# A gated two-branch decoder block on one core: another order for the gate products, the y pieces and the last output rows

## The chip, the cores and the metric

The kernel runs on one core of a Trainium2 chip. The metric is the device time of one execution in microseconds (us); the number given for a kernel is the median of several runs. The engines are PE (matrix products, with PEld for its weight loads), DVE (vector), ACT (scalar, activation functions), POOL (GpSimd) and SP, which in this kernel only issues DMAs. Each engine works through its own queue in order.

## The reference

The input x has 1024 rows of 1024 values. It is normalised and projected, two attention branches are computed, and they are merged by gates, cut here to what matters:

```python
h = rms_norm(x, g_pre)
qa, ka, va, fa, za, qb, kb, vb, zb, gates = split(h @ w_in)
ya = fox_attention(qa, ka, va, log_sigmoid(fa + b_forget))      # 8 heads, "forgetting"
ya = ya * silu(za)
yb = diff_attention(rope(qb), rope(kb), vb, lam)                # 4 heads, "differential"
yb = rms_norm(yb, g_subln) * (1 - lam_init) * silu(zb)
gate_a, gate_b = split(sigmoid(gates))                          # 1024 each
merged = gate_a * (ya @ w_branch[0]) + gate_b * (yb @ w_branch[1])
y = merged @ w_out
out = x + rms_norm(y, g_post)
```

All is float32. The kernel gets the accuracy by splitting each operand into a high and a low part and taking three products (high-high, high-low, low-high), so a product of 128x128 by 128x512 costs three matmuls per 128 of depth.

## The kernel before

The work has five stages. First x is normalised and transposed into hT (high and low parts, four quarters `hT[part][kh][sh]`: two halves of the model width by two halves of the rows), and the two value projections are taken. Then the attention stage runs eight units (four differential, four forgetting), with the projections for the next unit, the z projections and the row sums of squares as filling; what it makes for later goes to DRAM: y_d (the attention outputs, eight tiles of 128 channels: 0 to 3 differential, 4 to 7 forgetting), z_d, rs_d (the scale of the inner norm) and t_d (four combinations of quarters of h). The diff touches the three stages after that.

**Gates.** The 16 column blocks of the gate projection are made in eight steps d. Step 0 is plain (`gates_plain`): 96 matmuls. Steps 1 to 7 (`gates_pair`) take one block of each gate together by Winograd's form of Strassen's product: seven products of half size (`wino`, 84 matmuls) in place of eight. The left operands are the quarters a11, a12, a21, a22 of the two weight blocks, loaded as `raw` (a pool of two buffers, so the next pair's loads wait until this pair's are read), or combinations S1 to S4 of them (`left_operands`, on POOL). Product 1 takes a11, 2 takes a12, 4 takes a22; 5 takes S1, 6 takes S2, 3 takes S4 and 7 takes S3. Each left operand is split into its parts by ACT (high) and DVE or, for products 2 and 4, POOL (low), into one of six operand slots in turn (`whi`, `wlo`, `wop`, two each). The right operands of products 1, 2, 3 are quarters of hT, and those of 4 to 7 are the T tiles, which `h_load` brings back from t_d (1 MB each, eight of them). `ORD` is the order in which the products are taken; pair 7 has an order of its own. As products finish, DVE adds them up in tiles of the tag "t" (eight buffers, `tmp`), ACT takes the sigmoid, and SP stores the result in g_d.

Between the pairs stand pieces of y * silu(z) (`y_work(t, c)`: tile t, half c of the rows; silu(z) is z times sigmoid(z)): a load of z and, for the differential tiles, of the inner norm's scale, into "t" tiles; one more DVE pass for the differential tiles; a product on POOL, a sigmoid on ACT and a product on DVE. `YORD[d]` lists the pieces that follow pair d. `y_load` brings y back from y_d.

**Branch.** `yT` holds y in two parts (ACT and DVE). For the forgetting branch first (groups 2 and 3, tiles 4 to 7), then for the differential one, 8 blocks of w_branch are taken against it: 384 matmuls. DVE and POOL multiply by the gates and add into `mg`, 128 x 8 x 1024. The slots of yT's first two groups and mg lie where the T tiles were.

**Output.** `out_pair(i)` makes the output rows of blocks i and i + 4 by seven products, for i = 0 to 3; pairs 0 and 1 are interleaved. The left operands are column blocks of mg, `mg[:, 4*kh:4*kh+4, (i+4*n)*P : (i+4*n+1)*P]`. A result of 512 columns goes to `out_half`: ACT sums its squares, POOL (DVE for rows 3 and 7) multiplies by g_post, and when a row block's second half is there, POOL makes the reciprocal root (`rstd_of`: scale and offset, then a power) and DVE makes result times root plus the residual x. The residual comes by a DMA of its own into one of two "ox" buffers, or for rows 3 and 7 into `lx`.

**What sets the order.** The text is a list, and a planner (`schedule_with_timeline_sim=True`) puts each engine's instructions in order ahead of time: by its own model of durations, an engine takes the ready instruction that stands first in the text. So instructions run out of the text's order where the planner found one ready earlier; on the chip the planned order of each queue is fixed, and an instruction that waits holds everything behind it in its queue. An example from the trace: the weights of pair 7 (L802) are issued at 737 and 740 us, ahead of the last z loads of pair 6 (L765).

The lines that the prediction names: L664 and L665 split a left operand (high, low), L677 combines, L706 adds, L713 multiplies, L760 loads y, L765 loads z, L769 to L772 are the y pieces, L776 stores a gate, L795 loads T, L802 loads raw, L837 casts yT, L848 is the branch product, L931 loads a residual, L939 and L936 multiply by g_post, L943, L112 and L113 make the root, L948, L949 and L951 finish a row.

Of the kernel before, what the change touches and what calls it, by code (L numbers as in the profile page):

```python
# [16 lines left out]
P = 128  # L17
S = 1024
D = 1024
# [11 lines left out]
YORD = ((), ((0, 0),), ((0, 1), (1, 0)), ((1, 1), (2, 0)), ((2, 1), (4, 0), (4, 1)),  # L31
        ((3, 0), (5, 0), (5, 1)), ((3, 1), (6, 0), (6, 1), (7, 0), (7, 1)), ())
# [14 lines left out]
def tile_hybrid_block(  # L47
# [742 lines left out]
    def h_load():  # L790
        for m in (6, 5, 7, 4):
            ts = [tpool.tile([P, 4, CH], F32R, tag=f"T{m}{part}", name=f"T{m}{part}")
                  for part in range(2)]
            for part in range(2):
                nc.sync.dma_start(f32(ts[part]), t_d[m][part])  # L795
            h_ops[m] = [[t[:, k, :] for k in range(4)] for t in ts]
# [122 lines left out]
    last = NB - 1  # L919
    lx = []  # L920

    def out_half(i, e, o, st):

        es = slice(e * CH, (e + 1) * CH)
        if i in (3, last):
            if not lx:
                lx.append(slot(hslot[1, 1][0], [P, 4, CH], F32, "lx"))
            xs = lx[0][:, (0 if i == 3 else 2) + e]
        else:
            xs = tmp.tile([P, CH], F32, tag="ox", name=f"ox{i}_{e}", bufs=2)  # L930
        nc.sync.dma_start(xs, x2[i * P:(i + 1) * P, es])  # L931
        ss = small.tile([P, 1], F32, tag="oss", name=f"oss{i}_{e}")
        nc.scalar.activation(gx[:, 1, 0:CH], o, AF.Square, accum_out=ss)
        if i in (3, last):
            g = tmp.tile([P, CH], F32, tag="t", name=f"go{i}_{e}")
            nc.vector.tensor_tensor(g, o, gp_bc[:, es], op=ALU.mult)  # L936
        else:
            g = o
            nc.gpsimd.tensor_tensor(g, o, gp_bc[:, es], op=ALU.mult)  # L939
        st.append((e, g, xs, ss))  # L940
        if len(st) == 2:
            rs = small.tile([P, 1], F32, tag="ors", name=f"ors{i}")
            nc.gpsimd.tensor_tensor(rs, ss, st[0][3], op=ALU.add)  # L943
            rstd_of(rs, rs, D, EPS)
            for e, o, xs, _ in st:
                es = slice(e * CH, (e + 1) * CH)
                if i == 3 and e == 0:
                    nc.scalar.activation(o, o, AF.Copy, scale=rs)  # L948
                    nc.gpsimd.tensor_tensor(o, o, xs, op=ALU.add)  # L949
                else:  # L950
                    nc.vector.scalar_tensor_tensor(o, o, rs, xs, op0=ALU.mult, op1=ALU.add)  # L951
# [63 lines left out]
```

## Time and profile before

| what | us |
|---|---|
| median of 3 runs | 958.73 (956.02 to 959.63) |
| profiled execution | 960.13 |
| its span, first to last instruction | 958.0 |
| PE busy | 900.7 (94%) |
| DVE busy | 627.2 (65%) |
| POOL busy | 489.6 (51%) |
| ACT busy | 437.0 (46%) |
| first matmul of the gates | 603.2 |
| first matmul of pair 1 | 625.1 |
| first matmul of the branch | 768.4 |
| first matmul of the output | 859.6 |
| end of the last matmul | 939.4 |

The mean granted clock of PE over the span is 0.982 of full speed.

How to read the lines. In a timeline a line is: start, length, engine, line of the kernel, operation, output <- inputs by the program's names, shape, count of instructions merged into the line, and in brackets how long the engine sat idle just before and what ended that. SPq is SP's queue: the time of a DMA's issue, with the landing later. In a table of stretches a line is: from:to, its length, busy time and count of PE, PEld, DVE, ACT and POOL, then PE's granted clock, the share of the 16 DMA engines that was busy, and GB/s. In a table of groups a line is: line, engine, operation, output <- inputs, count, busy us, mean ns of one, and idle time before with what ended it.

### The profile page before, as it was taken

To read this page: it belongs to the slowest core of one execution; us is meant where nothing else is said; L and a number is where in the kernel's file an instruction comes from. 1 tells how busy PE (TensorE), PEld (TensorE's weight loads), DVE (VectorE), ACT (ScalarE), POOL (GpSimd) and SP (SyncE) were. 2 spreads that over 40 slices of the span, in tenths; PEclk is the share of its full clock that TensorE was granted. 3 is DMA by queue.
4 is the path that set the end of the run, shared out by engine and by line. 5 is a ranking of instruction groups with operands and counts; after the bars stand their busy time and mean duration, and the time that the engine had idled before them with its cause. 6 is when DMAs were issued, how large, how long until landed. Compare 5 with 4: busy or idle time off the path is not lost.

```text
span 958.0 us, 13760 instructions
## 1 busy us (share of the span) xinstructions
PE 900.7 (94%) x4600; PEld 752.1 (79%) x4600; DVE 627.2 (65%) x1180; ACT 437.0 (46%) x862; POOL 489.6 (51%) x460
## 2 busy tenths in 40 slices
PE   7999989899999999999999988999999999999992
PEld 5999867787887888888878877777888768887871
DVE  7731258978768868578676478228665782559875
ACT  3521125665656574565745658323443550324331
POOL 7200035446545466464644575216655735878972
PEclk9999999999999999999999999998999989999997
DMA  9532454434334353534434350893445696210144
GB/s 314 193 110 91 142 134 114 105 80 123 97 94 138 95 155 116 154 122 130 143 123 136 103 186 28 325 377 122 139 138 172 186 370 203 73 38 1 48 150 154
DMA packets 115656, 136.95 MB, mean 143 GB/s; under 512 B 10609, under 2 KB 80241, under 8 KB 114562
## 3 DMA queue, kind: packets, MB, share of 16 engines
q1 hardware_dynamic: 115586, 136.08, 44.4%
q8 instruction: 36, 0.59, 0.3%
q14 instruction: 34, 0.28, 0.1%
HBM read 85.65 MB, written 37.81 MB: 129 GB/s over the span
## 4 chain that ended last, share of the span: by engine, by line
PE 58%; DVE 13%; POOL 8%; DMA 7%; issue 6%; ACT 5%; SPq 2%; DVEq 0%; POOLq 0%; ACTq 0%
PE x_g L713 11%; PE pv L195 9%; PE pb L848 9%; PE pz L246 7%; PE pk L246 4%; PE pq L246 3%; PE ypf L474 3%; PE pg L246 2%; PE ptf L450 2%; DMA swk<-rawk 2%; SPq L287 1%; DVE Pd L423 1%; PE ypd L474 1%; PE Sf L421 1%; DVE wo_op L890 1%
## 5 line engine op out<-in xcount | busy, mean ns | idle before, releaser
L195 PE MATMUL pv<-wvhi,hT 128*128 128x264 f32 (+2 forms) x384 | 89.3, 325 | 0.4 <-DVE hT L181 0.4
L246 PE MATMUL pk<-hT,hi_k 128*128 128x512 f32 x256 | 83.9, 401 | 4.2 <-DVE KB L298 2.4
L246 PE MATMUL pz<-hT,hi_z 128*128 128x512 f32 x256 | 85.1, 400 | 0.0
L848 PE MATMUL pb<-yT,hi_br 128*128 128x512 f32 x256 | 80.8, 398 | 1.9 <-ACT hi_br L232 1.6
L246 PE MATMUL pq<-hT,hi_q 128*128 128x512 f32 x256 | 82.3, 395 | 0.0
L713 PE MATMUL x_g<-T,a_g 128*128 128x512 f32 x336 | 79.5, 392 | 1.6 <-ACT a_g L664 1.2
L713 PE MATMUL x_o<-wo_op,a_o 128*128 128x512 f32 x336 | 77.4, 391 | 2.4 <-ACT a_o L664 1.2
L713 PEld LDWEIGHTS x_o<-wo_op,a_o 128*128 128x128 f32 x336 | 62.8, 188 | 16.9 <-ACT a_o L664 2.1
L713 PEld LDWEIGHTS x_g<-T,a_g 128*128 128x128 f32 x336 | 63.5, 190 | 15.7 <-ACT a_g L664 1.6
L195 PEld LDWEIGHTS pv<-wvhi,hT 128*128 128x128 f32 x384 | 64.6, 190 | 6.2 <-DVE hT L181 0.7
L542 POOL TENSOR_SCALAR Pf<-Pf,lf 128x1024 f32<-128x1024 f32 (+3 forms) x64 | 52.5, 824 | 30.2 <-DVE lf L430 27.4
L713 PE MATMUL x_g<-hT,a_g 128*128 128x512 f32 x252 | 62.0, 400 | 2.6 <-ACT a_g L664 2.0
L428 ACT ACTIVATE Pf<-Pf,mxf 128x1024 f32<-128x1024 f32 (+3 forms) x64 | 49.8, 778 | 32.1 <-DVE mxf L423 29.5
L428 ACT ACTIVATE Pd<-Pd,mxd 128x128 f32<-128x128 f32 (+7 forms) x64 | 49.5, 774 | 30.0 <-DVE mxd L423 28.2
L538 POOL TENSOR_TENSOR cb<-cb,trim 128x128 f32<-128x128 f32 x64 | 30.0, 470 | 62.9 <-DVE mxf L423 45.1
L195 PE MATMUL pv<-wvlo,hT 128*128 128x512 f32 (+2 forms) x192 | 61.9, 325 | 0.0
L512 POOL TENSOR_SCALAR Pd<-Pd,ld 128x128 f32<-128x128 f32 (+7 forms) x32 | 25.6, 799 | 68.8 <-DVE ld L511 38.2
L848 PEld LDWEIGHTS pb<-yT,hi_br 128*128 128x128 f32 x256 | 49.1, 193 | 13.1 <-ACT hi_br L232 2.0
L713 PEld LDWEIGHTS x_g<-hT,a_g 128*128 128x128 f32 x252 | 48.5, 193 | 13.7 <-ACT a_g L664 2.4
L246 PEld LDWEIGHTS pk<-hT,hi_k 128*128 128x128 f32 x256 | 47.6, 190 | 14.4 <-DVE KB L298 2.5
L454 DVE TENSOR_TENSOR plf<-ptf,phf 128x512 fp32r<-128x512 f32 (+1 forms) x80 | 49.6, 633 | 10.1 <-ACT phf L453 9.5
L246 PEld LDWEIGHTS pz<-hT,hi_z 128*128 128x128 f32 x256 | 47.9, 191 | 8.7
(243 smaller groups left out, 2426.6 us busy)
## 6 DMA issues: line engine op xcount, KB each, us to landing
t_d<-t SPq DMA_DIRECT2D x32, 256.0 KB, 2.2
T<-t_d SPq DMA_DIRECT2D x8, 1024.0 KB, 14.9
raw<-in_w_in_dram SPq DMA_DIRECT2D x14, 512.0 KB, 4.1
g_d<-c_g SPq DMA_DIRECT2D x21, 256.0 KB, 3.9
vb_d<-vbs SPq DMA_DIRECT2D x8, 512.0 KB
va_d<-vas SPq DMA_DIRECT2D x8, 512.0 KB, 3.8
raw_k<-in_w_in_dram SPq DMA_DIRECT2D x8, 512.0 KB, 5.3
raw_q<-in_w_in_dram SPq DMA_DIRECT2D x8, 512.0 KB
```

The costliest lines, as they stand in the source:

```text
L195: nc.tensor.matmul(ps[n], lhsT=hT[hp][k // 4][i // 4][:, k % 4, hs], rhs=wt[k][:, a:b], start=first, stop=(k == KT - 1 and hp == 1))
L246: nc.tensor.matmul(ps, lhsT=a[:, k, :], rhs=hT[h][k // 4][c][:, k % 4, :], start=(k == 0 and a is hi and h == 0), stop=(k == KT - 1 and a ...
L287: nc.sync.dma_start(sw[b * 32:(b + 1) * 32, :], raw[o * 32:(o + 1) * 32, :])
L428: nc.scalar.activation(pr[:, 0:n], pr[:, 0:n], AF.Exp, bias=mx[:, len(pcs) - 1:len(pcs)], scale=-1.0, accum_out=le)
L450: nc.tensor.transpose(pt[:, o * P:(o + 1) * P], rows[2 * g + r][:, j * P:(j + 1) * P], ident)
L454: nc.vector.tensor_tensor(pl[:, 0:n], pt[:, 0:n], ph[:, 0:n], op=ALU.subtract)
L474: nc.tensor.matmul(o, lhsT=a, rhs=b[:, src], start=(j == 0 and n == 0), stop=(odd == 1 and jj == g and n == len(prods) - 1))
L512: nc.gpsimd.tensor_scalar(p2[:, 0:n], p2[:, 0:n], l2, 1.0, op0=ALU.mult, op1=ALU.mult)
L538: nc.gpsimd.tensor_tensor(diag, diag, trim, op=ALU.add)
L542: nc.gpsimd.tensor_scalar(p1[:, 0:n], p1[:, 0:n], l1, 1.0, op0=ALU.mult, op1=ALU.mult)
L713: nc.tensor.matmul(x[m], lhsT=a[:, ai, k, :], rhs=right[m][bi][k], start=(k == 0 and n == 0), stop=(k == 3 and n == 2))
L848: nc.tensor.matmul(ps, lhsT=a[:, kk, :], rhs=yT[g][h][:, k % 2, sl], start=(k == 0 and a is hi and h == 0), stop=(k == 3 and a is lo))
```

## The change

Four things are changed.

- Pairs 1 to 6 take their products in the order 1, 2, 4, 6, 5, 7, 3 (`GATE`) in place of 1, 6, 5, 7, 2, 3, 4, and the T tiles are loaded in the order 4, 6, 5, 7. Pair 7 keeps its order. Because product 2 now comes before 6, the sum of products 1 and 2 gets a tile of its own instead of going over c11.
- The y pieces stand in another order and number: 2, 3 and 3 pieces of the forgetting tiles after pairs 1, 2 and 3, then 3, 3 and 2 of the differential tiles after pairs 4, 5 and 6. Before it was 1, 2, 2, 3, 3 and 5, differential first. All eight y loads stand before pair 1, the forgetting tiles first.
- The residual rows 2, 6, 3 and 7 are loaded, one DMA each, into columns of mg that output pairs 0 and 1 have read, and their loads stand in the text before pair 2. Rows 0, 4, 1 and 5 keep the two ox buffers.
- The last output pair takes 1, 6, 5, 7, 3, 4, 2 in place of 1, 6, 5, 2, 3, 7, 4. The norm's factor is moved: g_post is multiplied by the root of 1024 once, the first half's sum of squares gets the offset, and what is left behind the second half is one addition and one power. In row 3 it is the half that came first that ACT and POOL finish.

```diff
-YORD = ((), ((0, 0),), ((0, 1), (1, 0)), ((1, 1), (2, 0)), ((2, 1), (4, 0), (4, 1)),
-        ((3, 0), (5, 0), (5, 1)), ((3, 1), (6, 0), (6, 1), (7, 0), (7, 1)), ())
+YORD = ((), ((4, 0), (4, 1)), ((5, 0), (5, 1), (6, 0)), ((6, 1), (7, 0), (7, 1)),
+        ((0, 0), (0, 1), (1, 0)), ((1, 1), (2, 0), (2, 1)), ((3, 0), (3, 1)), ())
...
     def h_load():
-        for m in (6, 5, 7, 4):
+        for m in (4, 6, 5, 7):
...
+    GATE = (1, 2, 4, 6, 5, 7, 3)
     h_load()
     gates_plain(0)
-    for t in range(4):
+    for t in (4, 5, 6, 7, 0, 1, 2, 3):
         y_load(t)
     for d in range(1, KT):
-        if d == 4:
-            for t in range(4, 8):
-                y_load(t)
-        gates_pair(d, ORD if d < KT - 1 else (7, 5, 6, 4, 1, 2, 3))
+        gates_pair(d, GATE if d < KT - 1 else (7, 5, 6, 4, 1, 2, 3))
...
+    nc.gpsimd.tensor_scalar(gp_bc, gp_bc, math.sqrt(D), 1.0, op0=ALU.mult, op1=ALU.mult)
+    xres = {}
+
+    def residual(i, e):
+        if i % 4 < 2:
+            xs = tmp.tile([P, CH], F32, tag="ox", name=f"ox{i}_{e}", bufs=2)
+            nc.sync.dma_start(xs, x2[i * P:(i + 1) * P, e * CH:(e + 1) * CH])
+            return xs.rearrange("p (k n) -> p k n", k=4)
+        return xres[i][:, 4 * e:4 * e + 4]
+
+    def residual_early(i):
+        xs = mg[:, :, (i - 2) * P:(i - 1) * P]
+        nc.sync.dma_start(xs, x2[i * P:(i + 1) * P, :].rearrange("p (k n) -> p k n", k=KT))
+        xres[i] = xs
...
+        if not st:
+            nc.gpsimd.tensor_scalar(ss, ss, D * EPS, 0.0, op0=ALU.add, op1=ALU.add)
         st.append((e, g, xs, ss))
         if len(st) == 2:
             rs = small.tile([P, 1], F32, tag="ors", name=f"ors{i}")
             nc.gpsimd.tensor_tensor(rs, ss, st[0][3], op=ALU.add)
-            rstd_of(rs, rs, D, EPS)
-            for e, o, xs, _ in st:
+            nc.gpsimd.tensor_tensor(rs, rs, mhalf[:, 0:1], op=ALU.pow)
+            for n, (e, o, xs, _) in enumerate(st):
                 es = slice(e * CH, (e + 1) * CH)
-                if i == 3 and e == 0:
+                o4 = o.rearrange("p (k n) -> p k n", k=4)
+                if i == 3 and n == 0:
                     nc.scalar.activation(o, o, AF.Copy, scale=rs)
-                    nc.gpsimd.tensor_tensor(o, o, xs, op=ALU.add)
+                    nc.gpsimd.tensor_tensor(o4, o4, xs, op=ALU.add)
                 else:
-                    nc.vector.scalar_tensor_tensor(o, o, rs, xs, op0=ALU.mult, op1=ALU.add)
+                    nc.vector.scalar_tensor_tensor(o4, o4, rs, xs, op0=ALU.mult, op1=ALU.add)
                 nc.sync.dma_start(out2[i * P:(i + 1) * P, es], o)
...
     run_all(out_pair(0, OORD), out_pair(1, OORD))
+    for i in (2, 6, 3, 7):
+        residual_early(i)
     run_all(out_pair(2, ORD))
-    run_all(out_pair(3, (1, 6, 5, 2, 3, 7, 4)))
+    run_all(out_pair(3, (1, 6, 5, 7, 3, 4, 2)))
```

More of the change, by code (lines that the diff above doesn't have):

```diff
@@ L918, in tile_hybrid_block @@
     nc.sync.dma_start(gp_bc, g_post[0:1].to_broadcast([P, D]))
-    last = NB - 1
-    lx = []
+    nc.gpsimd.tensor_scalar(gp_bc, gp_bc, math.sqrt(D), 1.0, op0=ALU.mult, op1=ALU.mult)
[10 more added lines that the diff above has]
+        xres[i] = xs
     def out_half(i, e, o, st):
         es = slice(e * CH, (e + 1) * CH)
[L925 to L931, printed above, removed]
+        late = i % 4 == 3
+        xs = residual(i, e)
         ss = small.tile([P, 1], F32, tag="oss", name=f"oss{i}_{e}")
         nc.scalar.activation(gx[:, 1, 0:CH], o, AF.Square, accum_out=ss)
-        if i in (3, last):
+        if late:
             g = tmp.tile([P, CH], F32, tag="t", name=f"go{i}_{e}")
```

## Prediction

> **What bounds the kernel now.** I read the page first, for the engine that fills the span, then PE's own timeline from the gates on, since the diff touches nothing earlier, then the rows of the engines that end PE's waits.
>
> ```profile
> span 958.0 us, 13760 instructions
> PE 900.7 (94%) x4600; PEld 752.1 (79%) x4600; DVE 627.2 (65%) x1180; ACT 437.0 (46%) x862; POOL 489.6 (51%) x460
> ```
>
> PE has work for 94% of the span. So only the holes in PE's stream, and the end after its last matmul, are to be had.
>
> ```profile
> 625.14 2.88 PE L713 MATMUL x_g<-hT,a_g 128*128 128x512 f32 x12
> 646.30 0.83 PE L713 MATMUL x_g<-hT,a_g 128*128 128x512 f32 x2 [1.95 <-ACT a_g L664]
> 647.82 4.63 PE L713 MATMUL x_g<-hT,a_g 128*128 128x512 f32 x10 [0.69 <-DVE a_g L665]
> 669.24 2.88 PE L713 MATMUL x_g<-hT,a_g 128*128 128x512 f32 x12
> 688.27 2.88 PE L713 MATMUL x_g<-hT,a_g 128*128 128x512 f32 x12
> 746.76 0.73 PE L713 MATMUL x_g<-T,a_g 128*128 128x512 f32 x2 [1.20 <-ACT a_g L664]
> 768.39 1.21 PE L848 MATMUL pb<-yT,hi_br 128*128 128x512 f32 x4 [1.62 <-ACT hi_br L232]
> 859.63 11.04 PE L713 MATMUL x_o<-wo_op,a_o 128*128 128x512 f32 x48
> 917.62 21.81 PE L713 MATMUL x_o<-wo_op,a_o 128*128 128x512 f32 x94 [1.15 <-POOL a_o L665]
> ```
>
> These are PE's rows: start, length, and in brackets the wait before. Pair 1 starts at 625.14, pair 3 at 669.24, pair 4 at 688.27. An undisturbed pair is 688.27 - 669.24 = 19.03 us for 84 matmuls, 0.2266 us each. Pairs 1 and 2 took 44.10 us, not 38.06: **6.0 us lost** (A). Pairs 4 to 7 should end at 688.27 + 4 x 19.03 = 764.39, and the branch starts at 768.39: **4.0 us lost** (B), in pair 7 (746.76) and at the handover. The branch's 384 matmuls take 87.0 us at that pace and took 859.63 - 768.39 = 91.2: **4.2 us lost** (C). PE's last run ends at 917.62 + 21.81 = 939.4, and the span runs **18.6 us** on (D).
>
> ```profile
> 625.10:644.10 19.00, 19.00 (x85) 15.58 (x84) 4.84 (x7) 4.62 (x8) 2.58 (x2) 1.00 1.04 384
> ...
> 644.00:648.00 4.00, 1.35 (x5) 0.48 (x4) 2.42 (x3) 2.41 (x5) 3.34 (x3) 0.85 0.67 252
> 648.00:652.00 4.00, 4.00 (x10) 3.13 (x11) 4.00 (x4) 1.00 (x2) 3.37 (x3) 0.50 0.00 0
> 652.00:656.00 4.00, 4.00 (x16) 3.20 (x15) 3.27 (x3) 2.14 (x4) 4.00 (x3) 0.80 0.06 8
> 744.00:748.00 4.00, 2.41 (x10) 1.35 (x9) 1.26 (x2) 1.24 (x2) 3.15 (x3) 1.00 0.62 207
> 772.00:776.00 4.00, 4.00 (x11) 3.03 (x11) 4.00 (x4) 2.19 (x3) 2.37 (x1) 0.50 1.04 380
> ```
>
> In these stretches the last three figures are the granted clock, the DMA share and GB/s, and x after the second time counts PE's matmuls. After the waits at 644 and 768 the clock is half for some us: 26 matmuls in 648 to 656 where 35 fit (2.1 us lost), 11 in 772 to 776 where 18 fit (1.5 us). After the shorter wait at 745 it stays at 1.00. So A and C are part waiting, part slow clock.
>
> **Part 1: products 1, 2, 4 first.** What ends the wait of pair 2?
>
> ```profile
> 629.24 1.29 POOL L665 TENSOR_TENSOR a_g<-raw,a_g 128x512 fp32r<-128x512 f32 x1 [1.14 <-ACT a_g L664]
> 623.45 7.76 SPq L760 DMA_DIRECT2D yf<-y_d  x4
> 634.07 3.32 SPq L802 DMA_DIRECT2D raw<-in_w_in_dram  x2
> 644.58 1.27 POOL L677 TENSOR_TENSOR S_g<-raw 128x512 f32<-128x512 f32 x1 [14.05 <-DMA raw<-in_w_in_dram]
> 738.56 1.30 POOL L665 TENSOR_TENSOR a_g<-raw,a_g 128x512 fp32r<-128x512 f32 x1 [1.18 <-ACT a_g L664]
> 739.89 0.38 SPq L802 DMA_DIRECT2D raw<-in_w_in_dram  x1
> 744.77 1.28 POOL L677 TENSOR_TENSOR S_g<-raw,raw 128x512 f32<-128x512 f32 x1 [4.91 <-DMA raw<-in_w_in_dram]
> ```
>
> The next weights wait for the two raw buffers, and these come free with the splits of a12 and a22, products 2 and 4, which stand fifth and last. A split needs one of six operand slots, so product 4's waits for product 1 of its own pair: 629.24 in pair 1, 738.56 in pair 6. The load goes out behind it, 739.89, and lands 4.9 us later; pair 7 should have begun at 745.4. In front, the three splits that read raw directly need the slots of the second to fourth product of the pair before, done 10.9 us into that pair. So raw comes free some 8 us before its own pair starts instead of some 12 us after the start (738.56, where pair 6 began at 688.27 + 2 x 19.03 = 726.33): about 20 us more lead. In pair 1 the slots come free in the middle of the plain gates, about 614, so pair 2's weights go out behind the T loads and ahead of the yf loads, where they now go out after both. I estimate their landing at 632 to 636; they are needed at 644. The split counts, combinations and additions are the same in number. T4 is needed third instead of T6 second; the loads follow that order. One more "t" tile is held per pair (the sum p12 no longer overwrites c11), 5 of 8.
>
> **Part 2: the y pieces.** The forgetting tiles are the branch's first operands, and their pieces are now the last.
>
> ```profile
> 761.21 1.74 POOL L770 TENSOR_TENSOR yf<-yf,zs 128x512 f32<-128x512 f32 x1
> 763.51 3.88 ACT L837 CAST yT<-yf 128x1024 fp32r<-128x1024 f32 x4
> 767.30 1.04 ACT L232 CAST hi_br<-raw_br 128x1024 fp32r<-128x1024 f32 x1
> ```
>
> The last yf product at 761.21 holds ACT's four casts, these hold hi_br, and hi_br is PE's wait at 768.39. Done by pair 4 or 5, the casts are free from T's last use, four products into pair 7: 8.2 us before the end, against 3.88 + 1.04 us of ACT. What is loaded more: pairs 5 to 7 get three pieces of the differential kind.
>
> ```profile
> L665 DVE TENSOR_TENSOR a_g<-S_g,a_g 128x512 fp32r<-128x512 f32 x23 | 26.5, 1159 | 20.2 <-ACT a_g L664 20.2
> L706 DVE TENSOR_TENSOR c_g<-x_g,cu_g 128x512 f32<-128x512 f32 x10 | 6.8, 684 | 0.2
> L769 DVE SCALAR_TENSOR_TENSOR yd<-yd,gsub,rb 128x512 f32<-128x512 f32 x7 | 8.0, 1149 | 0.0
> L772 DVE TENSOR_TENSOR yd<-yd,zs 128x512 f32<-128x512 f32 x8 | 9.8, 1223 | 2.6 <-ACT zs L771 2.4
> ```
>
> DVE per such pair: 5 x 1.16 + 7 x 0.68 + 3 x (1.15 + 1.22) = 17.7 us under 19.03 us of PE. It is hidden, with 1.3 us to spare; without that cover each pair would cost what it runs over. Of A + B + C = 14.2 us I keep back 1.2 for a handover that is not seamless: **-13.0** (bounds: -14.2, and -2 if only pair 7's own 2 us go). Moving the y loads costs nothing: the planner put the yf loads at 623 already, far from their place in the text.
>
> **Part 3: residual rows and the last pair.**
>
> ```profile
> 937.38 0.33 SPq L931 DMA_DIRECT2D ox<-in_x_dram  x1
> 942.93 0.75 DVE L951 SCALAR_TENSOR_TENSOR cu_o<-cu_o,ors,ox 128x512 f32<-128x512 f32 x1 [3.95 <-DMA ox<-in_x_dram]
> 948.24 0.72 ACT L948 ACTIVATE go<-go,ors 128x512 f32<-128x512 f32 x1 [1.21 <-POOL ors L113]
> 949.04 1.27 POOL L949 TENSOR_TENSOR go<-go,lx 128x512 f32<-128x512 f32 x1 [0.83 <-ACT go L948]
> 950.96 0.68 DVE L706 TENSOR_TENSOR cu_o<-x_o,cu_o 128x512 f32<-128x512 f32 x1
> 952.82 0.19 POOL L112 TENSOR_SCALAR ors<-ors 128x1 f32<-128x1 f32 x1
> 953.68 1.42 DVE L951 SCALAR_TENSOR_TENSOR go<-go,ors,lx 128x512 f32<-128x512 f32 x2 [1.30 <-POOL ors L113]
> ```
>
> DVE stood 3.95 us for a residual row that could only be issued at 937.38, when one of two ox buffers came free; all additions of the last pair stand behind it in DVE's queue, and the very last one starts at 950.96, 11.5 us after PE is done. From it to the end are 7.0 us. With rows 2, 6, 3 and 7 in columns of mg that pairs 0 and 1 have done with, nothing of that waits: those columns are read before pairs 0 and 1 end, 859.63 + 168 x 0.2266 and 1.2 us of waits, so by 899, and the rows are needed after pair 2, which ends 19 us before 939.4. Their loads move 512 KB each in 512-byte chunks, as the raw loads do, which land 4.9 us after issue; the passes read mg in chunks of 128, as the combinations of pairs 0 to 3 do. In the new order product 2 is last and finishes only row 3. The end after the last addition: 7.0, less one small POOL step (0.28), plus the first half by ACT and POOL (0.80 + 1.27) in place of two DVE passes (1.42): 7.4. Row 7's two DVE passes may stand ahead of the last addition, 1.4 us more; with 0.2 of queueing I take 9.0 for the 18.6: **-9.6** (bounds: 7.4, -11.2; and 18.6, nothing). The scaling of g_post on POOL is one pass of 128x1024, by the row below 1.3 us; before the first output it lies in POOL's wait for ACT, and if not, costs that much once.
>
> ```profile
> L234 POOL TENSOR_SCALAR hi_k<-raw_k 128x1024 fp32r<-128x1024 f32 x8 | 10.1, 1267 | 48.3 <-DMA vb_d<-vbs 48.3
> ```
>
> Products 4 and 2, split by POOL, are now needed at about 934 and 937 while POOL sums rows 2 and 6: I set **+1** (0 to 3).
>
> Sum: 958.0 - 13.0 - 9.6 + 1.0 = 936.4 us of span; 2.1 us lie around the span (the profiled execution took 960.13): 938.5. The median shown, 958.73, is 1.4 below the profiled one: **937 us**.
>
> **A rule against a part of it.** The rows show half clock right behind 2.6 us of waiting with two matmuls between. The Trainium skill (TensorE: Matmul & The Clock Gate, "What's actually happening") has the clock fall only after an idle window of about 3.4 us. By the rule the slow stretches would not come from these waits and would stay, 941. The rows at 744 (1.00) and 648 (0.50) speak for the wait as cause, with a threshold below the one of the Trainium skill.
>
> **The rivals.** (1) Forecast: A to D mostly go, 937, own range 930 to 944: 0.58. (2) Pair 2's weights still land behind T and yf, since DMA moves 384 GB/s up to 644: A stays, 937 + 6 = 943: 0.10. For it: the queue is full throughout (DMA share 1.04). Against it: pair 2's issue would come ahead of 2 MB of yf. (3) The tail stays, because DVE's order, fixed ahead of time by the planner, puts the last additions behind row passes anyway: 937 + 9.6 = 947: 0.13. (4) The half clock has another cause and stays, 2.1 us at 648 and 1.5 at 772: 941: 0.03. (5) The written order is only a priority and the planner restores about the same execution: 954 to 959: 0.07. (6) Slower: head of line on SP. Three differential pieces ask for 6 tiles beside the 5 of a pair, 11 through 8 buffers; a z load that waits for one holds the next pair's weights behind it, and a pair stalls as pair 2 did, 6.0 us. With the old holes left and only the tail gained that is 950 + 6 per pair, over 963 from three pairs on; with four, 974: 0.09. Against it: raw is now ready about 20 us earlier, so it should stand ahead of those z loads.
>
> This kernel's measurement tells about 0.5%, 4.8 us, from no change. Faster: 0.58 + 0.10 + 0.13 + 0.03 = 0.84; same 0.07; slower 0.09. The range 930 to 950 holds cases 1 to 4.
>
> **What would show it.** Right: pair 2 follows pair 1 in 19.0 us with clock 1.00 from 644 on; raw issues before 623 for pair 2 and some 20 us ahead later; the branch's first wait under 1.2 us; no DVE wait on a residual; PE's end to the span's end 8 to 10 us. Wrong: waits on zs or t buffers in front of raw on SP, DVE without gaps in pairs 5 to 7, or the last additions still long after PE's end.

## The result and the profile after

The changed kernel takes **945.99 us** (median of 4 runs, 944.34 to 950.13); the kernel before took 958.97 beside it (956.02 to 959.63). The ratio is 0.988, with a 95% interval of 0.985 to 0.991: faster by 13.0 us, where the forecast was 937, 21.7 us faster, with a range of 930 to 950. The profiled execution took 945.37, 2.1 us more than its span, as before.

The head of the page after:

```profile
span 943.3 us, 13785 instructions
PE 895.5 (95%) x4600; PEld 750.5 (80%) x4600; DVE 625.4 (66%) x1180; ACT 435.8 (46%) x862; POOL 489.3 (52%) x461
```

PE's own timeline after: pair 1's start, pair 7 (second and third rows), the handover to the branch, the output.

```profile
625.85 5.60 PE L713 MATMUL x_g<-hT,a_g 128*128 128x512 f32 x24
...
740.09 11.04 PE L713 MATMUL x_g<-T,a_g 128*128 128x512 f32 x48
750.97 8.32 PE L713 MATMUL x_g<-hT,a_g 128*128 128x512 f32 x36
...
759.13 1.52 PE L846 MATMUL pb<-yT,hi_br 128*128 128x512 f32 x6
760.99 0.50 PE L846 MATMUL pb<-yT,lo_br 128*128 128x512 f32 x1 [0.34 <-POOL lo_br L236]
...
846.81 11.04 PE L713 MATMUL x_o<-wo_op,a_o 128*128 128x512 f32 x48
...
899.59 5.78 PE L713 MATMUL x_o<-wo_op,a_o 128*128 128x512 f32 x24 [1.36 <-POOL a_o L665]
906.28 22.03 PE L713 MATMUL x_o<-wo_op,a_o 128*128 128x512 f32 x94 [0.92 <-POOL a_o L665]
```

No row between 625.85 and 759.13 has a wait: seven pairs in 133.28 us are 19.04 each. The stages, cut at these rows (columns as in the prediction's table of stretches; the clock is the third figure from the end):

```profile
625.85:759.13 133.28, 133.28 (x590) 110.40 (x588) 94.65 (x104) 58.32 (x99) 78.10 (x53) 1.00 0.65 207
759.13:846.81 87.68, 87.34 (x386) 72.02 (x384) 47.00 (x53) 23.80 (x29) 57.78 (x31) 1.00 0.51 171
846.81:928.31 81.50, 77.85 (x337) 62.50 (x335) 66.39 (x64) 27.98 (x57) 64.20 (x52) 1.00 0.29 90
928.31:943.30 14.99, 0.01 (x1) 0.00 (x0) 8.12 (x12) 3.61 (x9) 3.20 (x7) 0.60 0.20 76
```

Beside the kernel before, whose cuts come from the prediction's rows in the same way:

| stage | before, us | after, us | measured | forecast |
|---|---|---|---|---|
| gates, pairs 1 to 7 (A, B) | 143.25 | 133.28 | -9.97 | -10.0 |
| branch (C) | 91.24 | 87.68 | -3.56 | -4.2 |
| output, to PE's last matmul (E) | 79.80 | 81.50 | +1.70 | +1 |
| end, from there on (D) | 18.57 | 14.99 | -3.58 | -9.6 |
| sum from pair 1 on | 332.86 | 317.45 | -15.41 | -22.8; -21.6 with the 1.2 kept back |

Pair 1 starts 0.7 us later; in the runs below it starts anywhere from 623.9 to 630.3. So stages are compared by their lengths.

The gates and the branch came out as forecast. Nearly two thirds of the gain at the end did not come. DVE's timeline at the end, after:

```profile
916.62 0.68 DVE L706 TENSOR_TENSOR cu_o<-x_o,cu_o 128x512 f32<-128x512 f32 x1
920.30 3.46 DVE L962 SCALAR_TENSOR_TENSOR c_o<-c_o,ors,mg 128x512 f32<-128x512 f32 x2 [3.00 <-POOL ors L954]
924.47 1.77 DVE L962 SCALAR_TENSOR_TENSOR c_o<-c_o,ors,mg 128x512 f32<-128x512 f32 x1 [0.71 <-POOL ors L954]
926.16 0.74 DVE L962 SCALAR_TENSOR_TENSOR cu_o<-cu_o,ors,mg 128x512 f32<-128x512 f32 x1
926.83 0.68 DVE L706 TENSOR_TENSOR cu_o<-x_o,c_o 128x512 f32<-128x512 f32 x1
...
934.31 1.42 DVE L962 SCALAR_TENSOR_TENSOR go<-go,ors,mg 128x512 f32<-128x512 f32 x2 [1.12 <-POOL ors L954]
935.64 0.69 DVE L706 TENSOR_TENSOR c_o<-x_o,c_o 128x512 f32<-128x512 f32 x1
```

The old wait for a residual (3.95 us) is gone; two shorter ones, of 1.25 us at 909.88 and 0.61 us at 912.44, stay in output pair 2, for rows that still come through an ox buffer. In place of the old one DVE stands 3.00 and 0.71 us for the roots of rows 2 and 6, which POOL makes, and the four finishing passes of these rows (L962) come ahead of the last pair's **first** addition at 926.83. That is 1.5 us before PE's end, when six of the last pair's seven products are there. The last addition starts at 935.64, 7.3 us after PE's end, and from it to the end are 7.7 us (forecast 7.4).

Two theories stood for that end. The queue: DVE takes its instructions in the planned order, and the additions stand behind passes that wait for POOL; put behind, the end falls to 8 or 9 us. The rival: DVE or POOL has simply too much to do there, and its order does not matter.

### The profile page after: what moved, and what is told of

Read it like the earlier page. It is cut to its first block, busy times and chain, and to the rows that moved or that the text cites. A ratio compares the mean times of both kernels' runs of the same rounds, so it can differ in the third digit from the quotient of the medians.

```text
span 943.3 us, 13785 instructions
## 1 busy us (share of the span) xinstructions
PE 895.5 (95%) x4600; PEld 750.5 (80%) x4600; DVE 625.4 (66%) x1180; ACT 435.8 (46%) x862; POOL 489.3 (52%) x461
## 5 line engine op out<-in xcount | busy, mean ns | idle before, releaser
L846 PE MATMUL pb<-yT,hi_br 128*128 128x512 f32 x256 | 78.5, 389 | 0.0
L713 PE MATMUL x_g<-T,a_g 128*128 128x512 f32 x336 | 77.5, 389 | 0.0
L246 PEld LDWEIGHTS pk<-hT,hi_k 128*128 128x128 f32 x256 | 48.3, 193 | 14.5 <-DVE KB L298 2.4
L713 PE MATMUL x_g<-hT,a_g 128*128 128x512 f32 x252 | 58.6, 389 | 0.0
L246 PEld LDWEIGHTS pq<-hT,hi_q 128*128 128x128 f32 x256 | 47.5, 189 | 8.9
```

The lines of the kernel that those rows point to most:

```text
L246: nc.tensor.matmul(ps, lhsT=a[:, k, :], rhs=hT[h][k // 4][c][:, k % 4, :], start=(k == 0 and a is hi and h == 0), stop=(k == KT - 1 and a ...
L713: nc.tensor.matmul(x[m], lhsT=a[:, ai, k, :], rhs=right[m][bi][k], start=(k == 0 and n == 0), stop=(k == 3 and n == 2))
L846: nc.tensor.matmul(ps, lhsT=a[:, kk, :], rhs=yT[g][h][:, k % 2, sl], start=(k == 0 and a is hi and h == 0), stop=(k == 3 and a is lo))
```

## The experiments

All stage lengths below are cut as above, at the first matmul of pair 1, of the branch and of the output, the end of PE's last row, and the span's end. "Sum" is the four together. The ratio is to the kernel before in the same comparison, whose median was 958.16, 958.78, 957.19 and 957.36 in the four comparisons: rows 1 to 4, 5 to 8, 9 to 11, and the last. The stages are those of one profiled execution per kernel, the medians those of 4 to 10 executions. The kernel before was profiled in an execution 1.4 us above its median, and by the sums every row gains more than by the medians, 0.3 to 5.4 us more.

| kernel | gates | branch | output | end | sum | median, us | ratio (95% interval) |
|---|---|---|---|---|---|---|---|
| gate order alone | 135.78 | 91.21 | 79.79 | 18.71 | 325.49 | 954.19 | 0.994 (0.992 to 0.996) |
| y pieces alone | 144.99 | 87.04 | 79.77 | 18.93 | 330.73 | 958.67 | 1.000 (0.998 to 1.002) |
| output part alone | 141.03 | 88.92 | 81.46 | 14.95 | 326.36 | 956.35 | 0.998 (0.996 to 0.999) |
| after, constant for two roots | 133.28 | 87.81 | 81.10 | 14.33 | 316.52 | 944.48 | 0.985 (0.983 to 0.987) |
| after, passes put behind | 133.28 | 88.37 | 81.17 | 8.91 | 311.73 | 938.87 | 0.979 (0.976 to 0.982) |
| after, buffer alone | 133.28 | 87.38 | 80.75 | 14.98 | 316.39 | 945.79 | 0.986 (0.983 to 0.989) |
| after, old last pair | 133.28 | 87.29 | 82.62 | 11.32 | 314.51 | 941.52 | 0.982 (0.979 to 0.985) |
| gate order and y pieces | 133.28 | 88.12 | 79.78 | 19.52 | 320.70 | 946.88 | 0.988 (0.985 to 0.991) |
| old last pair, passes put behind | 133.28 | 88.34 | 80.64 | 9.51 | 311.77 | 940.72 | 0.982 (0.981 to 0.983) |
| passes put behind, DVE splits | 133.28 | 87.43 | 79.77 | 10.85 | 311.33 | 941.08 | 0.982 (0.980 to 0.984) |
| y pieces, pair 6 in the new order | 142.59 | 91.10 | 79.78 | 18.78 | 332.25 | 958.47 | 1.001 (0.999 to 1.003) |
| residuals of six rows early | 133.27 | 87.05 | 79.63 | 8.90 | 308.85 | 937.83 | 0.979 (0.975 to 0.982) |

### Each part alone

**The gate order alone.**

```diff
-        for m in (6, 5, 7, 4):
+        for m in (4, 6, 5, 7):
...
-        gates_pair(d, ORD if d < KT - 1 else (7, 5, 6, 4, 1, 2, 3))
+        gates_pair(d, GATE if d < KT - 1 else (7, 5, 6, 4, 1, 2, 3))
```

> The kernel before with part 1 alone: pairs 1 to 6 in the order 1, 2, 4, 6, 5, 7, 3 and the T loads in the order 4, 6, 5, 7. Theory (the raw buffers come free about 20 us earlier, each wait carries its own slow clock): pair 2 follows pair 1 without a wait and at clock 1.00 (6.0 us back), pair 7 without a wait (2 us back); the handover to the branch stays late with its slow clock, because the last forgetting pieces still end it. Span 950, 8 us below before. Rival (the pieces on POOL are what delays pair 7's weights): only 6 us back, 952.

Measured: the pairs run in 19.04 us each without a wait, and the handover to the branch is worse. PE's timeline of this run:

```profile
766.09 1.22 PE L849 MATMUL pb<-yT,hi_br 128*128 128x512 f32 x4 [2.33 <-ACT hi_br L232]
```

Pair 7 ends in time, so PE now stands longer for the casts that the five last y pieces hold up. A and pair 7's part of B belong to the gate order; the handover does not. The sum is 7.4 us below that of the kernel before, where 8 were expected (6 by the rival); the median is only 4.0 lower.

**The y pieces alone.**

```diff
-YORD = ((), ((0, 0),), ((0, 1), (1, 0)), ((1, 1), (2, 0)), ((2, 1), (4, 0), (4, 1)), ...
+YORD = ((), ((4, 0), (4, 1)), ((5, 0), (5, 1), (6, 0)), ((6, 1), (7, 0), (7, 1)), ...
```

> The kernel before with part 2 alone: the new order and number of the y pieces, all y loads ahead of pair 1. Theory: the branch starts without a wait and without a slow clock (1.8 and 4.2 us back), pair 2's stall of 6.0 us and its slow clock stay; span 952. Rival (the pieces also delay pair 7's weights): pair 7's 2 us come back too, span 950. Rival (the slow clock near 772 has another cause than the handover's wait): 956.

Measured: no gain at all. PE's timeline, at pair 7 and the handover:

```profile
747.82 13.04 PE L713 MATMUL x_g<-T,a_g 128*128 128x512 f32 x48 [2.74 <-ACT a_g L664]
...
768.86 1.52 PE L845 MATMUL pb<-yT,hi_br 128*128 128x512 f32 x6
```

The handover's wait is gone and the branch takes 87.04 us, so the forecast of that step holds. But pair 7 waits 2.74 us in place of 1.20, and runs 13.04 us for 48 matmuls that take 11.04 in the kernel after. POOL's timeline in this run, in front of that wait:

```profile
737.25 1.30 POOL L770 TENSOR_TENSOR yd<-yd,zs 128x512 f32<-128x512 f32 x1 [0.63 <-DVE yd L769]
740.28 1.29 POOL L665 TENSOR_TENSOR a_g<-raw,a_g 128x512 fp32r<-128x512 f32 x1 [1.73 <-ACT a_g L664]
745.86 1.26 POOL L677 TENSOR_TENSOR S_g<-raw,raw 128x512 f32<-128x512 f32 x1 [4.28 <-DMA raw<-in_w_in_dram]
```

The split that frees pair 6's last raw buffer comes at 740.28, behind a y piece and a cast, and pair 7's weights come after it. That the differential pieces in pairs 4 to 6 delay the late weights is read from this order and not tried by itself; the next run, in which the weights are no longer late, fits it. The branch's gain and pair 7's loss leave the median as it was, which no expectation had.

**Both together, with the old output.**

```diff
-        for m in (6, 5, 7, 4):
+        for m in (4, 6, 5, 7):
...
-        gates_pair(d, ORD if d < KT - 1 else (7, 5, 6, 4, 1, 2, 3))
+        gates_pair(d, GATE if d < KT - 1 else (7, 5, 6, 4, 1, 2, 3))
...
-YORD = ((), ((0, 0),), ((0, 1), (1, 0)), ((1, 1), (2, 0)), ((2, 1), (4, 0), (4, 1)), ...
+YORD = ((), ((4, 0), (4, 1)), ((5, 0), (5, 1), (6, 0)), ((6, 1), (7, 0), (7, 1)), ...
```

> The order of the gate products and the spread of the y pieces together, the output stage as in the kernel before. Theory (the two help one another: alone they gave 4.0 and 0 us, since the earlier weights leave pair 7 unstalled that the y pieces would otherwise stall): gates 133.3 and branch 87.7 us as in the changed kernel, output 79.8, end 18.6, about 947.5 us, 10.7 us under the kernel before. Rival (the effects simply add, and the rest of the gain comes from the output part): 953 to 954 us.

Measured: 946.88 against 958.78, 11.9 us, where the two alone gave 4.0 and -0.5 in their comparison. They are not additive (by the sums of stages it is 12.2 us, where the two alone gave 7.4 and 2.1): the gate order takes the weights out of the y pieces' way, and the y pieces take away the handover that the gate order exposes. The end is 19.52 us, 18.57 before.

**The y pieces and the new order in pair 6 only**, which should free pair 7's weights and nothing else.

```diff
-        gates_pair(d, ORD if d < KT - 1 else (7, 5, 6, 4, 1, 2, 3))
+        gates_pair(d, GATE if d == 6 else ORD if d < KT - 1 else (7, 5, 6, 4, 1, 2, 3))
```

> The y pieces alone, and in pair 6 only the products in the order 1, 2, 4, 6, 5, 7, 3, so that pair 7's weights can be loaded earlier; pairs 1 to 5 and the rest as in the run of the y pieces alone, where pair 7 lost 2.7 us of waiting and about 2.3 us of slow clock and the whole came out even. Theory (pair 7's weights, late behind pair 6's splits, ate what the handover gained): pair 7 starts without a wait, gates 140 in place of 145.0 us, branch 87.0 and no wait ahead of it, pair 2's stall stays, 953 to 954.5 us. Rival (the y pieces load DVE and POOL so that pair 7's own splits are late in any order): pair 7's wait stays over 2 us, 957.5 to 959.

Measured: 958.47, where 953 to 954.5 were expected; the theory's time was wrong. Its first step held: pair 7 starts without a wait. But pair 6 now waits for POOL's split of product 4, and the handover's wait came back. PE's timeline, then ACT's and SP's of the same run:

```profile
731.99 10.74 PE L713 MATMUL x_g<-T,a_g 128*128 128x512 f32 x46 [1.13 <-POOL a_g L665]
...
745.92 11.05 PE L713 MATMUL x_g<-T,a_g 128*128 128x512 f32 x48
...
767.64 1.28 PE L846 MATMUL pb<-yT,hi_br 128*128 128x512 f32 x4 [2.51 <-ACT hi_br L232]
```

```profile
762.22 0.63 ACT L771 ACTIVATE zs<-zs 128x512 f32<-128x512 f32 x1 [1.67 <-POOL yd L770]
762.76 3.88 ACT L835 CAST yT<-yf 128x1024 fp32r<-128x1024 f32 x4
766.54 1.04 ACT L232 CAST hi_br<-raw_br 128x1024 fp32r<-128x1024 f32 x1
```

```profile
749.73 0.94 SPq L228 DMA_DIRECT2D raw_br<-in_w_branch_dram  x2
750.76 0.44 SPq L765 DMA_DIRECT2D zs<-z_d  x1
751.73 0.42 SPq L765 DMA_DIRECT2D zs<-z_d  x1
```

The z loads of the last two pieces stand on SP behind the branch's weights, which could only be issued at 749.73. So their sigmoids stand at 759.9 and 762.22 in ACT's queue, ahead of the casts of yT. In the kernel after, the same two queues, ACT and SP:

```profile
752.43 0.64 ACT L771 ACTIVATE zs<-zs 128x512 f32<-128x512 f32 x1 [1.67 <-POOL yd L770]
752.97 3.89 ACT L835 CAST yT<-yf 128x1024 fp32r<-128x1024 f32 x4
756.76 1.04 ACT L232 CAST hi_br<-raw_br 128x1024 fp32r<-128x1024 f32 x1
```

```profile
740.11 0.94 SPq L228 DMA_DIRECT2D raw_br<-in_w_branch_dram  x2
741.15 0.44 SPq L765 DMA_DIRECT2D zs<-z_d  x1
742.16 0.38 SPq L765 DMA_DIRECT2D zs<-z_d  x1
```

The order is the same, some 10 us earlier, and hi_br is done at 757.80, 1.3 us before PE asks for it at 759.13. That is all the slack there is.

**The output part alone.**

```diff
-    run_all(out_pair(3, (1, 6, 5, 2, 3, 7, 4)))
+    for i in (2, 6, 3, 7):
+        residual_early(i)
...
+    run_all(out_pair(3, (1, 6, 5, 7, 3, 4, 2)))
```

The scaled g_post and the split root belong to it too.

> The kernel before with part 3 alone: early residual rows, the new last order, the shorter root. Theory from the changed kernel's trace: PE's end to the span's end 15.0 in place of 18.6, the output products 1.7 longer by waits for POOL's splits; span 956, 1 to 3 us below before. Rival (the parts help one another, the output gains more or less when the gates are unchanged): outside 954 to 958.

Measured: output and end together 96.41 us in place of 98.37, and a median 1.8 us lower. The end is 14.95, as in the kernel after: it doesn't depend on the gates.

### The end

**A constant for the roots of rows 2 and 6.**

```diff
-nc.vector.scalar_tensor_tensor(o4, o4, rs, xs, op0=ALU.mult, op1=ALU.add)
+nc.vector.scalar_tensor_tensor(o4, o4, mhalf[:, 0:1] if i in (2, 6) else rs, xs, op0=ALU.mult, op1=ALU.add)
```

> The changed kernel with the row passes of rows 2 and 6 multiplied by a constant that is there from the start, in place of their reciprocal root; the output of these rows is not the reference's. The passes stay on DVE, their number too; only their wait for POOL's root is gone. Theory (the last pair's additions stand behind these four passes in DVE's queue, and the passes wait for POOL): DVE's waits of 3.0 and 0.7 us at 920 to 925 go, the first addition of the last pair starts before 923 in place of 926.8, span 939 to 940. Rival (DVE has simply too much work at the end): span 943 as now.

Measured: end 14.33 us, 0.7 less; the first addition starts at 928.25. By its numbers the rival came out. DVE's timeline shows another reason:

```profile
926.43 1.91 DVE L962 SCALAR_TENSOR_TENSOR cu_o<-cu_o,mhalf,mg 128x512 f32<-128x512 f32 x1 [2.96 <-POOL cu_o L947]
```

Without the root the pass waits 2.96 us for POOL's product with g_post, which stands ahead of the root in POOL's queue. What holds DVE there is POOL's chain for row 6 up to that product, not only the small root steps. So this run does not tell the two theories apart; the next does.

**The passes put behind.** Rows 2, 6 and 7 are finished behind g_post products of the last pair, and the products have a buffer of their own.

```diff
+    BEHIND = {2: (7, 1), 6: (3, 1), 7: (3, 0)}
...
-    run_all(out_pair(3, (1, 6, 5, 7, 3, 4, 2)))
+    for _ in out_pair(3, (1, 6, 5, 7, 3, 4, 2)):
+        for i, go in BEHIND.items():
+            if i in later and go in gos:
+                with tc.issue_after(gos[go].ins):
+                    later.pop(i)()
...
-            g = tmp.tile([P, CH], F32, tag="t", name=f"go{i}_{e}")
+            if not gq:
+                gq.append(slot(hslot[1, 1][0], [P, 4, CH], F32, "gq"))
+            g = gq[0][:, (0 if i == 3 else 2) + e]
```

> The changed kernel with one more change: on DVE the finishing passes of rows 2, 6 and 7 are put behind the g_post products of the last pair (row 7's second, row 3's second, row 3's first half), and these products go to a buffer of their own so that they need no "t" tile. The work is the same. Theory (the end is long because the last pair's additions stand behind row passes that wait for POOL's roots): the first addition of the last pair starts at its product, about 10 us earlier than 926.8, the last one within 1 us of PE's end, from PE's end to the span's end 8 to 9 us in place of 15.0, PE's stages as in the changed kernel, 939 to 940 us, 0.980 of the kernel before. Rival 1 (DVE or POOL is simply overloaded at the end, the order does not matter): end 14 to 15 us, 945 to 946. Rival 2 (an in-order queue only moves the wait: the additions pass, but the row passes and stores of rows 2 and 6 are then late themselves): end 11 to 13 us, 942 to 944.

> Control to the run before: only the buffer for the g_post products of rows 3 and 7, DVE's order as in the changed kernel. If the order is what counts, end 15.0 us and 946 us. If instead the lack of "t" tiles held the last additions, end 9 to 12 us and 940 to 943.

Measured: with the order, the end is 8.91 us and the time 938.87; with the buffer alone, 14.98 and 945.79. DVE's first and last addition of the last pair, in the run with the order:

```profile
918.30 0.69 DVE L706 TENSOR_TENSOR cu_o<-x_o,c_o 128x512 f32<-128x512 f32 x1 [1.32 <-ACT c_o L716]
...
928.60 0.68 DVE L706 TENSOR_TENSOR c_o<-x_o,c_o 128x512 f32<-128x512 f32 x1
```

PE ends at 928.09 there. The additions begin 9.8 us before that, in place of 1.5, and the last one starts 0.5 us behind it, in place of 7.3. The work is the same and only the order differs, so the order of the queue is shown to be the cause of the 6 us, and the rival falls. DVE has no listed wait from 918.30 to 931.34, and the last pass of row 6 starts at 926.62, hardly later than in the kernel after (926.16). The waits of 3.71 us for the roots are gone, and the four passes of rows 2 and 6 take 2.9 us in place of 6.0; why they are shorter was not tried. The run also moves row 7's two passes behind the last addition, so the 6.1 us belong to both moves; each alone was not tried.

**The old order of the last pair**, in the kernel after, and then with the passes put behind.

```diff
-    run_all(out_pair(3, (1, 6, 5, 7, 3, 4, 2)))
+    run_all(out_pair(3, (1, 6, 5, 2, 3, 7, 4)))
```

> The changed kernel with the last pair in the old order of products (1, 6, 5, 2, 3, 7, 4); early residual rows and moved factor stay. Theory (the last pair's additions begin only when row 6's passes are done, whatever the order, and all but the last product are then there): end 14 to 16 us, PE's output stage within 1 us of 81.5, 945 to 947 us. Rival (the new order is worth what the prediction gave it, one store chain in place of two behind the last product): end 17 us or more, 948 to 950. Other rival (the new order costs 1 to 2 us of PE, since POOL's splits of products 4 and 2 come late): output stage 80 us, 944.

> The last pair in the old order of products (1, 6, 5, 2, 3, 7, 4), with the finishing passes of rows 2, 6 and 3 put behind the g_post products of row 3's first, row 3's second and row 7's first half on DVE, and the buffer for these products: what the run with the passes put behind does, for the old order. It asks what the new order is worth once no addition waits behind a row pass. Theory (without those waits the end is the chain behind the last addition, which is about as long in both orders, so the 2.6 us by which the old order won in output and end together, 93.9 against 96.5, came from the queue): last addition within 1.5 us of PE's end, end 9 to 10 us, output stage 82.6 as with the old order before, together 91.5 to 92.5 against 90.1 for the new one, 940 to 941 us. Rival (the old order is better in itself, by its earlier finish of row 3): together 87.5 to 89, 936 to 938.

Measured: in the kernel after, the old order is better: end 11.32, output and end together 93.94 against 96.49, and 941.52 us. That was in none of the expectations. By the medians of one comparison the gap is 4.3 us (941.52, and 945.79 with the buffer alone, which ends like the kernel after). DVE's timeline of this run:

```profile
924.62 0.68 DVE L706 TENSOR_TENSOR cu_o<-x_o,c_o 128x512 f32<-128x512 f32 x1
...
932.56 0.68 DVE L706 TENSOR_TENSOR cu_o<-x_o,cu_o 128x512 f32<-128x512 f32 x1
```

PE ends at 928.38. The additions begin 3.8 us before it and the last one starts 4.2 us behind it: POOL has one split of the last pair less between row 2's and row 6's chains, and DVE is free sooner. With the passes put behind, the old order's output and end are 90.15 us together (91.5 to 92.5 expected) and the new one's 90.08: equal. So the new order brings nothing by itself, and costs 2.6 us where the queue holds the additions. That is rather too little: in the old order's profiled execution the output stage holds a stretch of slow clock (0.64 from 904 to 908) behind a wait of 2.60 us, which makes PE's last row 1.4 us longer than in the kernel before (23.17 and 21.81 us for the same 94 matmuls).

**DVE's splits in output pair 2**, on top of the passes put behind: PE's waits for POOL there (1.07 and 0.95 us).

```diff
-            split(t, v, nc.gpsimd if m in (2, 4) else nc.vector)
+            split(t, v, nc.gpsimd if m in (2, 4) and nm != "o2" else nc.vector)
```

> The run with the passes put behind, and in output pair 2 DVE takes the low-part splits of products 2 and 4 in place of POOL, for which PE waited 1.07 and 0.95 us there. Theory (POOL, which sums rows at that time, is what is late): both waits go or fall under 0.4 us, output stage 79 to 79.7 in place of 81.2, end unchanged 8.9, 936.5 to 937.5 us. Rival (the splits now stand behind DVE's row passes, which wait 4.1 us for a root and 1.8 us for a residual): PE waits grow to 2 us or more, output stage 82 or more, 940 us or more.

Measured: the output stage shortens to 79.77 as expected, but the end grows to 10.85, which was not, so the two together hardly change (90.62, 90.08 in the run before). DVE's first and last addition of the last pair:

```profile
920.52 0.69 DVE L706 TENSOR_TENSOR cu_o<-x_o,c_o 128x512 f32<-128x512 f32 x1 [1.32 <-ACT c_o L716]
...
930.50 0.68 DVE L706 TENSOR_TENSOR c_o<-x_o,c_o 128x512 f32<-128x512 f32 x1
```

They start at about the same distance from each other (9.98 us, 10.30 in the run with the passes put behind). PE ends at 928.05, so the first starts 7.5 us before that in place of 9.8, and the last one 2.5 us behind it in place of 0.5.

**The residuals of rows 1 and 5 early too**, which should let that chain start sooner.

```diff
-        if i % 4 < 2:
+        if i % 4 < 1:
...
-        xs = mg[:, :, (i - 2) * P:(i - 1) * P]
+        xs = mg[:, :, (i - 1) * P:i * P]
```

> The run with DVE's splits in output pair 2 and the passes put behind, and in addition the residuals of rows 1 and 5 too are loaded into columns of mg that pair 0 has read (rows 2 and 6 then take those of pair 1, rows 3 and 7 those of pair 2), so that only rows 0 and 4 use the two ox buffers. There, DVE waited 0.47 and 1.15 us for a residual near 910 and began the last pair's additions 8 us before PE's end, and its last addition stood 2.4 us behind PE's end. Theory (the last addition is late because DVE's chain is pushed back by residuals in ox): no wait on an ox load after 900, last addition within 1 us of PE's end, end 9 to 9.5 us, output stage 79.8, together 88.7 to 89.3 against 90.6 and 90.1, 937 to 939.5 us. Rival (DVE's own work in the last pair, some 10 us without a gap behind ACT's copy of product 1, sets the end): last addition still 2 us or more late, together 90 or more, 940 to 941 us.

Measured: PE ends at 909.32 + 18.88 = 928.20, and the last addition starts 0.6 us later. No wait for an ox buffer's load is left after 900, so the residuals were what pushed the chain back. PE's last row and DVE's last addition:

```profile
909.32 18.88 PE L713 MATMUL x_o<-wo_op,a_o 128*128 128x512 f32 x82 [0.29 <-DVE a_o L665]
```

```profile
928.83 0.68 DVE L706 TENSOR_TENSOR c_o<-x_o,c_o 128x512 f32<-128x512 f32 x1
```

Output and end take 88.53 us together (expected 88.7 to 89.3). At 937.83 us this is the fastest kernel of the study: 19.5 us under the kernel before, and 8 under the changed one by medians. Against the passes put behind alone, the intervals overlap; only the stages tell them apart, output and end by 1.55 us (the branch, which neither change touches, differs by another 1.3).

## Why the prediction was right or wrong

**The gates (A, B): right, in amount and in place.** Forecast 10.0 us, measured 9.97. SP's timeline after, with the weights of pair 2 (the first two rows), y, and the weights of pair 7:

```profile
619.19 0.38 SPq L802 DMA_DIRECT2D raw<-in_w_in_dram  x1
...
631.43 0.43 SPq L802 DMA_DIRECT2D raw<-in_w_in_dram  x1
...
634.91 2.82 SPq L760 DMA_DIRECT2D yf<-y_d  x4
...
717.58 2.09 SPq L802 DMA_DIRECT2D raw<-in_w_in_dram  x2
```

Pair 2's weights go out ahead of the yf loads as forecast, the second one later than "before 623" but early enough. Pair 7's go out from 717.6, where they went out at 737 and 740. These 20 us are not the forecast lead of 20: pair 6 itself now starts at 721.05 in place of 726.33. Against that start the loads go out 3.5 us ahead in place of 11 and 14 us behind, a lead of about 15 us (8 us ahead were forecast), and that is enough. Two more things in the working were too simple. A and B were summed as separate gains; in the gates stage the gate order alone gave 7.5 us and the y pieces alone lost 1.7. And "the casts are free from T's last use" isn't what sets them: T is last read at about 751, but the casts begin behind the last sigmoid, 752.97.

**DVE's load in pairs 5 to 7: right that it hides, sized too high.** Forecast 17.7 us under 19.03 of PE; in the kernel after DVE is busy 15.7, 16.1 and 14.5 us in pairs 5, 6 and 7, and no pair waits.

**The branch (C): right in amount, its reason only half.** Without the handover's wait the half clock was gone and 3.56 of 4.2 us came; the rest is 0.34 us of waiting and a little at its sides. But a wait of that length isn't always followed by half clock (the last section), so a part of the amount, and of A's, is luck of the execution that was profiled. In the nine executions that have the new gates and y pieces the branch takes 87.05 to 88.37 us, with up to 0.93 us of waiting for POOL's part of w_branch (lo_br).

**The end (D): wrong.** Forecast -9.6, measured -3.58. The step that failed is "with 0.2 of queueing I take 9.0 for the 18.6". By it the last addition starts 1.6 us after PE's end; it starts 7.3 us after it. The step counted row 7's two passes ahead of the last addition, at 1.4 us (with the wait for their root they stand 2.5 us ahead of it), and not the four passes of rows 2 and 6 ahead of the first one. Taking the residual's wait away left DVE standing at the same place for POOL's root, as the third rival had it. DVE's rows before show waits for these same two roots already, at the first pass of row 2 and of row 6; the third line is the last pair's first addition:

```profile
932.81 1.77 DVE L951 SCALAR_TENSOR_TENSOR c_o<-c_o,ors,ox 128x512 f32<-128x512 f32 x1 [1.00 <-POOL ors L113]
935.58 1.77 DVE L951 SCALAR_TENSOR_TENSOR c_o<-c_o,ors,ox 128x512 f32<-128x512 f32 x1 [1.00 <-POOL ors L113]
...
938.30 0.68 DVE L706 TENSOR_TENSOR cu_o<-x_o,c_o 128x512 f32<-128x512 f32 x1
```

The third line stands ahead of the residual's wait at 942.93, so six of the last pair's seven additions stood behind it, and not all as the prediction has it. The third rival priced the loss at all of the 9.6; it was 6.1 (8.9, the end with the passes put behind, against 15.0). The measured 946 lies in the stated range but outside the forecast's own 930 to 944, and next to this rival's 947; so near a hit of that number is luck, since the 3.6 us that the end did gain are made up for by other terms (the sum below). The chain behind the last addition was right: 7.4 forecast, 7.66 measured. The new order of the last pair, taken as a part of the gain, cost 2.6 us.

**The splits (E): size about right, place wrong.** Forecast +1 for products 4 and 2 late in output **pair 3**. Measured +1.70, but PE's waits for POOL (1.36 and 0.92 us) are in **pair 2**, at 899.59 and 906.28. The kernel before had one there, of 1.15 us, so the waits grew by 1.13; the rest of the 1.70 lies in the rows around them, which are longer for the same matmuls (the row of 94 took 22.03 us in place of 21.81). The old last order has an even longer output stage (82.62, 1.4 of it slow clock) with a wait of 2.60 us for POOL in pair 2, so the early residuals and the moved factor play a part; that they do it by POOL's planned order was not tried.

**The others.** Pair 2's late weights (943) and an order restored by the planner (954 to 959) did not come about. A half clock of another cause (941) didn't either: the stage rows after show 1.00 up to PE's end. The sixth, loads held behind others on SP, cost nothing in the changed kernel; it did cost time, in another place, in the run with pair 6 alone in the new order, where z loads stood behind the branch's weights.

In sum: A, B, C and E make -11.83 us where -12.0 were forecast, D -3.58 where it was -9.6, and pair 1 starts 0.7 later: 936.4 + 0.2 + 6.0 + 0.7 = 943.3, the span. The median is 9.0 us over the forecast of 937: 6.9 in the span, 1.4 that the forecast took off the profiled time by the kernel before, and 0.6 by which the changed kernel's median stands above its own profiled time (the rest is rounding).

## What to carry to other kernels

When a wait is taken away from an in-order queue, look at what stands next in that queue and what it needs: here the wait for a residual gave way, at the same place, to one for POOL's chain, and only moving the waiting instructions back in the queue gave the 6 us. Gains at one handover aren't additive either: by medians the gate order and the y pieces gave 4.0 and -0.5 us alone and 11.9 together, by the sums of stages 7.4, 2.1 and 12.2. A new order of products is worth nothing by itself where its results are held up behind it; the queue comes first.

## What the runs showed of the hardware

**The same wait can end in half clock or not.** Granted clock after PE's waits, from the stretches of 4 us:

| where | waits, us | lowest clock of a stretch |
|---|---|---|
| before, pair 2 | 1.95, 0.69 | 0.50 |
| output part alone, pair 2 | 1.95, 0.55 | 0.76 |
| y pieces with pair 6, pair 2 | 1.95, 0.93 | 1.00 |
| before, handover | 1.62, 0.27, 0.42 | 0.50 |
| output part alone, handover | 1.64, 0.27, 0.91 | 1.00 |
| y pieces with pair 6, handover | 2.51, 0.20, 0.41 | 0.57 |
| y pieces alone, pair 2 | 1.95, 0.71 | 0.50 |
| y pieces alone, pair 7 | 2.74 | 0.57 |
| gate order alone, handover | 2.33, 0.27, 0.42 | 0.50 |
| before, pair 7 | 1.20, 0.39 | 1.00 |
| after, old last pair: output pair 2 | 2.60 | 0.64 |
| old last pair, passes put behind: output pair 2 | 2.17 | 1.00 |

Two of these stretches, first of the output part alone (the handover), then of the run with pair 6 (pair 2):

```profile
772.00:776.00 4.00, 3.31 (x15) 2.75 (x16) 4.00 (x5) 3.38 (x4) 1.81 (x2) 1.00 1.05 394
```

```profile
648.00:652.00 4.00, 4.00 (x18) 3.31 (x19) 4.00 (x3) 2.67 (x5) 4.00 (x3) 1.00 0.00 1
```

In the kernel before, the stretches from the same places show 0.50. So from pair 1 on no waiting under 2.3 us in all was followed by a slow stretch in these runs, and waiting of 2.3 us or more was in some places and not in others: C's 4.2 us is the price of one execution, and the branch took 88.92 us, not 91.2, in the run of the output part with nearly the same wait (1.64 us). The Trainium skill (TensorE: Matmul & The Clock Gate, "What's actually happening") says that activity is watched in a free-running window, so that the same kernel differs from run to run by the window's phase. The rows agree with the phase. They don't agree with the idle window of about 3.4 us that it asks for: 2.74 us of waiting were enough.

**A stage that nothing touched moves by 4 us.** Eight kernels of the table and the changed one have the same text up to the output, and their gates agree within 0.01 us; yet pair 1 starts at 624.00 in one execution and at 628.25 in another. A change of 2 us in a later stage is seen in that stage's length, and not in the time of one execution.
